# Two-layer mixer block in split fp32: partial-array products of a group issued without others between them, and another table of steps

## Chip, cores and metric

One core of a Trainium2 chip runs the whole block. The metric is the device time of one execution in microseconds. Three executions of the kernel before took 908.3, 911.97 and 912.93 us, with a median of 911.97 us.

## What is computed

Two layers over 256 tokens of width 1024, batch 1, all in fp32. A layer normalises x, multiplies by `w_in` and feeds three mixers: attention with 8 heads over compressed keys and queries (MLA), gated linear attention with 4 heads in chunks of 64 tokens (GLA), and a diagonal state-space mixer (S5) with 32 groups of 16 channels and 64 complex states each. Their outputs are gated and merged, go through `w_out`, and a feed-forward part with squared ReLU follows.

```python
for l in range(DEPTH):                       # 2
    z = rms_norm(x, norm1_g[l]) @ w_in[l]
    (cq, ckv, kpe, gq, gk, gv, glr, gr, su, gates) = split_in(z)
    o_a = mla_mixer(cq, ckv, kpe, ...)
    o_b = gla_mixer(gq, gk, gv, glr, gr, ...)
    o_c = s5_mixer(su, ...)
    g = sigmoid(gates + gate_b[l]).reshape(B, L, 3, D)
    merged = g[:,:,0]*(o_a@w_br_mla[l]) + g[:,:,1]*(o_b@w_br_gla[l]) + g[:,:,2]*(o_c@w_br_s5[l])
    x = x + merged @ w_out[l]
    x = x + square(relu(rms_norm(x, norm2_g[l]) @ w_ff1[l])) @ w_ff2[l]
```

## The kernel before

Every large product keeps fp32 accuracy by three products of rounded halves (`mm3`, L178 to L181): hi by hi, hi by lo, lo by hi. Weights stream in 128x1024 chunks (`raw`, by the SP queue); ScalarE rounds each into `hi` (L159) and VectorE takes the rest into `lo` (L160). These products use the whole 128x128 array.

The smaller products are plain fp32, and the hardware runs each such matmul of the program as two, so that a program's matmul is two in the trace (transposes are one). Several use only a part of the array:

- `s5_v` (L565 to L574): the S5 inputs `V`. 16 matmuls per call, two calls per layer (steps `v0`, `v2`). Each uses 64 of the 128 rows; those of strip 0 use the upper half of the rows and those of strip 1 the lower half, and the two halves can run side by side. A call takes all four PSUM tiles of the pool `acc`.
- `gla_core`, first part (L941 to L953): `Ap`, 8 matmuls per layer on 64 rows, in two halves as above. Third part (L975 to L998): `glo`, on 64 columns or on 64 rows by 64 columns. Between them `dS` (L967), in quarters of the array.
- `att_pv` (L856 to L877): after every second head, four matmuls into `po`, two heads on 64 columns each.
- `s5_y` (L610 to L637): `yp`, one product with `K` on the whole array, then 16 on 32 columns each, for each of four channel tiles; four strips of 32 columns can run side by side.

The order of the program is not written out. A layer's mixers are cut into steps (`table`, L1160), and `STEPS` (L1142) lists them, one string per layer; `P` is a part of `s5_pre` (layer 0 alone: layer 1's parts run in the feed-forward part of layer 0), and `~n` moves a step's priority by n instructions. A scheduler then places each instruction on its engine by its priority and by when it believes its operands and buffers to be ready. So it also puts whole-array products between those of one partial group. What it has written out, each engine then runs in order.

The names in the rows: `gp` are the products of the gates, `cp` those of the latents, `brp` of the branches, `fp` and `fo` of the feed-forward part, `s` and `PTp` scores and transposed probabilities of a head, `hT` and `goT` transposes. A shape like 64*128 is rows by columns of the array, and 64x128 what streams through.

Of the kernel before, what the change touches and what calls it, by code (L numbers as in the profile page):

```python
# [20 lines left out]
L = 256  # L21
NT = L // 128
# [15 lines left out]
# Columns of w_in by part.  # L38
# [7 lines left out]
# Weight chunks, one row of the packed array each: (name, columns used).  # L46
# [12 lines left out]
# Columns of the packed small parameters.  # L59
# [9 lines left out]
# Columns of the packed constants.  # L69
# [17 lines left out]
class Kern:  # L87
# [100 lines left out]
    def ws4(self, outs, ws):  # L188
        """Four column tiles; the second half of the rows comes last."""
# [25 lines left out]
    def exp(self, y, x, n):  # L215
        """exp of a small [128, n] tile: 2^k times the series of the rest."""
# [10 lines left out]
        # k + 127 in the lowest bits, shifted to where the exponent is  # L227
# [4 lines left out]
    def split(self, hi, lo, src, scale=None):  # L232
        """hi + lo == src * scale"""
# [80 lines left out]
    def s5_pre(self, l):  # L314
# [22 lines left out]
        # in turns of the two steps of a chunk: thi + tlo, thi with few enough bits for exact products  # L337
# [12 lines left out]
        # lam_bar, (lam_bar - 1) / lam  # L350
# [20 lines left out]
        # b_bar, lam_bar b_bar, c lam_bar; each comes without its zeros and is copied into a block-diagonal form  # L371
# [11 lines left out]
        def cmul(outr, outi, ar, ai, xr, xi, neg=False):  # L383
            """(xr + i xi)(ar + i ai); with neg the second output is negated"""
# [20 lines left out]
        # first row of a chunk: lam_bar b_bar, second: b_bar  # L405
# [19 lines left out]
        # operands of the input products  # L425
# [11 lines left out]
        # within a chunk  # L437
# [12 lines left out]
        # angle of the rotation by chunk  # L450
# [80 lines left out]
    def norm_rows(self):  # L531
        """The tokens' factors along the columns, in every row."""
# [32 lines left out]
    def s5_v(self, l, r):  # L565
        """The input products of two strips: they hold different rows of the array."""
        nc, s = self.nc, self.s5c[l]
        self.V = [[self.pt(f"V{i}", [128, 4, 128], tag="acc") for i in range(2)] for _ in range(2)]
        for i in range(2):
            for q in range(4):  # L570
                for rr in range(2):
                    rows = slice(64 * rr, 64 * rr + 64)
                    nc.tensor.matmul(self.V[rr][i][:, q, :], lhsT=s["Bt"][i][rows, 2 * q + r // 2, :],
                                     rhs=self.u2[r // 2][rows, q, :], start=True, stop=True)  # L574

    def s5_r(self, l, r):
# [17 lines left out]
        # the running sum, chunk by chunk of the four tiles (R is 0 at each first chunk)  # L594
# [5 lines left out]
        # the states take the place of this strip's cosines and sines  # L600
# [7 lines left out]
    def s5_y(self, l):  # L608
# [5 lines left out]
        for i in range(2):  # L614
            p = self.pt("yp", [128, 2, L])
            for qq in range(2):
                q = 2 * i + qq
                st = [slice(32 * r, 32 * r + 32) for r in range(4)]
# [737 lines left out]
```

## Time and profile before

| | |
|---|---|
| runs | 908.3, 911.97, 912.93 us; median 911.97 |
| the profiled execution | span 909.6 us; what lies around the span is not given, so the span stands for its own time |
| TensorE busy | 892.9 us, 98% of the span |
| VectorE / ScalarE busy | 674.7 us (74%) / 518.8 us (57%) |
| DMA | 147.78 MB, mean 162 GB/s |
| layer 0, mixers and `w_out` | about 12 to 270 us; feed-forward to about 460 us |
| layer 1 | mixers from about 460 us; feed-forward from about 720 us |

The profile counts TensorE as busy while any matmul is in flight, and matmuls overlap, so a busy share near 100% does not say how fast it goes. The distance from one start to the next does. The granted clock (PEclk) is 1.00 or 0.50 of 2.4 GHz in any one instant; a mean in between is a mix of the two.

### The profile page before, as it was taken

What the parts mean: (1) busy time and instruction counts of PE and PEld (TensorE: products, weight loads), DVE (VectorE), ACT (ScalarE), POOL (GpSimd) and SP (SyncE); (2) the same over time, 40 slices, a digit from 0 to 9 for tenths busy, and PEclk for the clock granted to TensorE, in tenths of its full rate; (3) what the DMA queues carried; (4) which work ended last, traced back from release to release, by engine and by line L of the source; (5) the groups of instructions that cost most, each with busy time, mean ns of one, the idle gap of its engine ahead of it and who ended that gap; (6) DMA issues with size and microseconds to landing.
All of it is one profiled execution on the core that took longest, in us unless ns stands there. A gap on an engine that the chain in (4) does not pass through costs nothing.

```text
span 909.6 us, 16218 instructions
## 1 busy us (share of the span) xinstructions
PE 892.9 (98%) x6428; PEld 813.0 (89%) x6428; DVE 674.7 (74%) x1283; ACT 518.8 (57%) x794; POOL 19.7 (2%) x35
## 2 busy tenths in 40 slices
PE   7999999999999999999999999999999999999998
PEld 6879988899989999999898899879999899999996
DVE  7999999977777966875686777968878765555554
ACT  6777888545555655654457557744445554444442
POOL 2000000010000000000000000000000000000000
PEclk9999999999999999999999999978999999999999
DMA  7535434346665565666645345323555556666662
GB/s 260 177 110 150 144 116 124 91 147 207 193 200 164 175 197 178 189 188 185 185 154 170 111 152 151 105 70 116 163 163 181 173 184 189 190 191 188 186 186 93
DMA packets 42266, 147.78 MB, mean 162 GB/s; under 512 B 4688, under 2 KB 5328, under 8 KB 42192
## 3 DMA queue, kind: packets, MB, share of 16 engines
q1 hardware_dynamic: 42192, 146.76, 52.3%
q8 instruction: 50, 0.82, 0.4%
q14 instruction: 24, 0.20, 0.1%
HBM read 145.70 MB, written 1.05 MB: 161 GB/s over the span
## 4 chain that ended last, share of the span: by engine, by line
PE 86%; DVE 5%; ACT 4%; DMA 2%; issue 1%; SPq 0%; ACTq 0%; DVEq 0%
PE fp L179 7%; PE fp L181 7%; PE fp L180 7%; PE fo L179 6%; PE fo L180 6%; PE fo L181 6%; PE gp L179 4%; PE gp L180 4%; PE gp L181 4%; PE brp L179 2%; PE brp L181 2%; DVE lo L160 2%; PE brp L180 2%; PE wo L179 2%; PE wo L180 2%; PE wo L181 2%
## 5 line engine op out<-in xcount | busy, mean ns | idle before, releaser
L160 DVE TENSOR_TENSOR lo<-raw,hi 128x1024 fp32r<-128x1024 f32 (+1 forms) x276 | 333.1, 1208 | 157.0 <-ACT hi L159 156.0
L159 ACT CAST hi<-raw 128x1024 fp32r<-128x1024 f32 (+1 forms) x276 | 286.0, 1037 | 285.3 <-PE fp L180 81.3
L179 PE MATMUL fp<-h,hi 128*128 128x256 f32 x512 | 145.2, 284 | 0.0
L180 PE MATMUL fp<-h,hi 128*128 128x256 f32 x512 | 145.0, 283 | 0.0
L181 PE MATMUL fp<-h,lo 128*128 128x256 f32 x512 | 144.9, 283 | 0.0
L179 PE MATMUL gp<-h,hi 128*128 128x256 f32 x384 | 112.0, 295 | 0.2 <-DVE gt L1043 0.2
L181 PE MATMUL gp<-h,lo 128*128 128x256 f32 x384 | 111.1, 292 | 0.0
L180 PE MATMUL gp<-h,hi 128*128 128x256 f32 x384 | 110.7, 291 | 0.0
L179 PE MATMUL fo<-hi,r 128*128 128x512 f32 x256 | 100.2, 391 | 0.0
L180 PE MATMUL fo<-lo,r 128*128 128x512 f32 x256 | 99.9, 390 | 0.0
L181 PE MATMUL fo<-hi,r 128*128 128x512 f32 x256 | 99.6, 389 | 0.0
L179 PEld LDWEIGHTS fp<-h,hi 128*128 128x128 f32 x512 | 98.2, 192 | 0.9
L180 PEld LDWEIGHTS fp<-h,hi 128*128 128x128 f32 x512 | 98.2, 192 | 0.9
L181 PEld LDWEIGHTS fp<-h,lo 128*128 128x128 f32 x512 | 98.2, 192 | 0.0
L179 PEld LDWEIGHTS gp<-h,hi 128*128 128x128 f32 x384 | 74.1, 194 | 3.0 <-issue 1.6
L180 PEld LDWEIGHTS gp<-h,hi 128*128 128x128 f32 x384 | 74.3, 195 | 2.0 <-issue 1.3
L181 PEld LDWEIGHTS gp<-h,lo 128*128 128x128 f32 x384 | 74.2, 195 | 2.1 <-issue 1.4
L181 PEld LDWEIGHTS fo<-hi,r 128*128 128x128 f32 x256 | 48.1, 188 | 10.2
L179 PEld LDWEIGHTS fo<-hi,r 128*128 128x128 f32 x256 | 48.2, 188 | 9.2
L180 PEld LDWEIGHTS fo<-lo,r 128*128 128x128 f32 x256 | 48.2, 188 | 8.9
L1046 ACT ACTIVATE gt<-gt,hgateb 128x256 f32<-128x256 f32 x48 | 21.7, 500 | 11.9 <-DVE gt L1043 11.9
L180 PE MATMUL wo<-lo,mh 128*128 128x512 f32 x64 | 25.3, 395 | 0.0
(403 smaller groups left out, 1820.5 us busy)
## 6 DMA issues: line engine op xcount, KB each, us to landing
raw<-wst SPq DMA_DIRECT2D x266, 512.0 KB, 3.9
raw<-wst SPq DMA_DIRECT2D x6, 384.0 KB, 3.0
x<-xin SPq DMA_DIRECT2D x4, 256.0 KB, 4.9
raw<-wst SPq DMA_DIRECT2D x4, 256.0 KB, 5.5
bc_raw<-bcin SPq DMA_DIRECT2D x4, 256.0 KB, 3.9
out_dram<-x SPq DMA_DIRECT2D x4, 256.0 KB, 2.0
par<-parin SPq DMA_DIRECT2D x2, 205.0 KB, 6.4
masks<-consts SPq DMA_DIRECT2D x1, 128.0 KB, 4.1
```

The costliest lines, as they stand in the source:

```text
L159: nc.scalar.copy(hi[:, h], raw[:, h])
L160: nc.vector.tensor_tensor(out=lo[:, h], in0=raw[:, h], in1=hi[:, h].bitcast(F32), op=ALU.subtract)
L179: mm(out, lhsT=lt[0], rhs=rt[0], start=start, stop=False)
L180: mm(out, lhsT=lt[0], rhs=rt[1], start=False, stop=False)
L181: mm(out, lhsT=lt[1], rhs=rt[0], start=False, stop=stop)
L1046: nc.scalar.activation(g[:, m, :], g[:, m, :], AF.Tanh, scale=0.5, bias=self.small[l]["gateb"][:, c:c + 1])
```

## The change

A helper, `together()`, opens a block in which TensorE's instructions keep the order in which they are written. It is put around `s5_v`, the first and third parts of `gla_core`, the products of `att_pv`, and those of `s5_y`. Inside, the order is written anew, the halves in turns and the higher one first. `glo` of the first token tile is one whole-array product instead of two of 64 columns. `s5_y` has both `K` products first and then walks the four strips. Both strings of `STEPS` are new. The comments are gone, and lines move by some 5 to 8. Cut to its core:

```diff
+    def together(self):
+        return self.tc.manual_schedule(engines={mybir.EngineType.PE})
...
     def s5_v(self, l, r):
-        for i in range(2):
-            for q in range(4):
-                for rr in range(2):
+        with self.together():
+            for i in (1, 0):
+                for q in range(4):
+                    for rr in (1, 0):
...
     def s5_y(self, l):
-            for qq in range(2):
-                q = 2 * i + qq
-                mm(p[:, qq, 0::2], lhsT=s["K0"][:, q, :], rhs=self.u[:, q, 0::2], start=True, stop=False)
-                for i2 in range(2):
-                    for r in range(4):
-                        mm(p[st[r], qq, 2::2], lhsT=C[2 + i2][:, q, r, :], rhs=X[i2][:, r, q, 0:127],
-                           start=False, stop=i2 == 1)
-                for i2 in range(2):
-                    for r in range(4):
-                        mm(p[st[r], qq, 1::2], lhsT=C[i2][:, q, r, :], rhs=X[i2][:, r, q, :],
-                           start=i2 == 0, stop=i2 == 1)
+            with self.together():
+                for qq in range(2):
+                    q = 2 * i + qq
+                    mm(p[:, qq, 0::2], lhsT=s["K0"][:, q, :], rhs=self.u[:, q, 0::2], start=qq == 0, stop=False,
+                       skip_group_check=True)
+                for c, x in (((1, slice(1, L, 2)), slice(0, 128)), ((3, slice(2, L, 2)), slice(0, 127))):
+                    for i2 in range(2):
+                        for qq in range(2):
+                            for r in range(4):
+                                q = 2 * i + qq
+                                mm(p[st[r], qq, c[1]], lhsT=C[c[0] - 1 + i2][:, q, r, :], rhs=X[i2][:, r, q, x],
+                                   start=False, stop=i2 == 1, skip_group_check=True)
...
     def att_pv(self, l, h):
-        for k in range(2):
-            for j, x in enumerate((self.PT0, PT)):
+        with self.together():
+            for k in range(2):
+                for j, x in ((1, PT), (0, self.PT0)):
...
     def gla_core(self, l):
-        for t in range(NT):
-            ts_ = slice(t * 128, (t + 1) * 128)
-            for m in range(2):
-                for o in range(2):
+        with self.together():
+            for t in range(NT):
+                ts_ = slice(t * 128, (t + 1) * 128)
+                for m in range(2):
+                    for o in (1, 0):
...
-                if t:
-                    for o in range(2):
-                        mm(p[o], lhsT=A[o], rhs=vh[o], start=True, stop=False)
-                else:
-                    for o in range(2):
-                        for n in range(2):
-                            mm(p[o][half[n]], lhsT=A[o][:, half[n]], rhs=vh[o], start=True, stop=n == 0)
-                for n in (2 * t, 2 * t + 1):
-                    if n:
+        with self.together():
+            for t in range(NT):
+                for m in range(2):
+                    c = (t * 2 + m) * 128
                     for o in range(2):
+                        h = (2 * m + o) * 128
+                        mm(self.gpo[o][:, t, m, :], lhsT=self.At[o][:, c:c + 128], rhs=self.gv[t][:, h:h + 128],
+                           start=(t, m) == (0, 0), stop=False, skip_group_check=True)
+            for n in range(1, 4):
+                for m in range(2):
...
     STEPS = [
-        "qk P~-60 kg P~60 P~-75 P~-30 gate~30 P P~-2 P gv su0 P su0~-30 gv~27 gv gv core P ckv core~-30 P~-30 "
+        "qk P~-60 kg P~68 P~-15 gv~42 gate~30 P P~-2 P~15 gv su0 P P~-30 su0~-30 gv gv core~-8 ckv core~-98 P "
...
```

What it moves, in three places. TensorE in layer 1, the second call of `s5_v` (`V`, strips 2 and 3), before:

```order
L573 MATMUL V_7062<-u_6547,Bt 128x128 x2
L179 MATMUL gp<-h_5302,hi 128x256
L573 MATMUL V_7064<-u_6547,Bt 128x128 x2
L180 MATMUL gp<-h_5303,hi 128x256
L573 MATMUL V_7062<-u_6547,Bt 128x128
L573 MATMUL V_7064<-u_6547,Bt 128x128
L181 MATMUL gp<-h_5302,lo 128x256
L573 MATMUL V_7062<-u_6547,Bt 128x128
L179 MATMUL gp<-h_5302,hi 128x256
L573 MATMUL V_7064<-u_6547,Bt 128x128
L180 MATMUL gp<-h_5303,hi 128x256
```

and with the change, where the two tiles of one component take turns four times, and then those of the other:

```order
L185 MATMUL gp<-h_5329,hi 128x256
L186 MATMUL gp<-h_5328,lo 128x256
L579 MATMUL V_7170<-u_6580,Bt 128x128
L579 MATMUL V_7168<-u_6580,Bt 128x128
...
L579 MATMUL V_7169<-u_6580,Bt 128x128
L579 MATMUL V_7167<-u_6580,Bt 128x128
...
L184 MATMUL gp<-h_5328,hi 128x256
```

Twelve places at which a product of the gates (or a transpose `PTp`) stood between two `V` are gone; at least ten products of the gates in a row now stand ahead of the group.

TensorE in layer 1, the first part of `gla_core`, before:

```order
L180 MATMUL gp<-h_5303,hi 128x256
L950 MATMUL Ap<-ep,en 128x128
L181 MATMUL gp<-h_5302,lo 128x256
L950 MATMUL Ap<-ep,en 128x128
L179 MATMUL gp<-h_5302,hi 128x256
L950 MATMUL Ap<-ep,en 128x128
L180 MATMUL gp<-h_5303,hi 128x256
```

and so on for eight `Ap`; with the change:

```order
L184 MATMUL gvp<-hi,h_5328 128x512
L185 MATMUL gvp<-lo,h_5328 128x512
L186 MATMUL gvp<-hi,h_5329 128x512
L960 MATMUL Ap<-ep,en 128x128 x8
L184 MATMUL gp<-h_5328,hi 128x256
```

All eight stand together. TensorE in layer 0, the second call of `s5_v`, before (the scores `s` of one head ahead of it):

```order
L840 MATMUL s<-kT,qT 128x128
L840 MATMUL s<-kT,qT 128x256
L573 MATMUL V_2047<-u_1479,Bt 128x128
L573 MATMUL V_2049<-u_1479,Bt 128x128
...
L862 MATMUL PTp<-con,ppt 128x128
L573 MATMUL V_2049<-u_1479,Bt 128x128
L573 MATMUL V_2048<-u_1479,Bt 128x128
L862 MATMUL PTp<-con,ppt 128x128 x2
```

and with the change:

```order
L848 MATMUL s<-kT,qT 128x128
L848 MATMUL s<-kT,qT 128x256
L848 MATMUL s<-kT,qT 128x128
L848 MATMUL s<-kT,qT 128x256
L579 MATMUL V_2093<-u_1515,Bt 128x128
L185 MATMUL gp<-h_96,hi 128x256
L579 MATMUL V_2091<-u_1515,Bt 128x128
...
L579 MATMUL V_2092<-u_1515,Bt 128x128
L186 MATMUL gp<-h_95,lo 128x256
...
L579 MATMUL V_2090<-u_1515,Bt 128x128
```

Here the block only keeps the order of its own products: others still stand between them, at two places, and the scores of two heads stand directly ahead.

## Rows read from the trace of the kernel before

**Rows 1.** The page: its first line, the busy time, share and instructions of TensorE, and the shares of the chain of work that ended last, by engine.

```profile
span 909.6 us, 16218 instructions
...
PE 892.9 (98%) x6428; PEld 813.0 (89%) x6428; DVE 674.7 (74%) x1283; ACT 518.8 (57%) x794; POOL 19.7 (2%) x35
...
PE 86%; DVE 5%; ACT 4%; DMA 2%; issue 1%; SPq 0%; ACTq 0%; DVEq 0%
```

**Rows 2.** Timeline of TensorE in layer 1, the beginning of the `Ap` group. Columns: start in us, length in us, engine, line, operation, tiles, array rows*columns, what streams, count.

```profile
493.18 0.28 PE L179 MATMUL gp<-h,hi 128*128 128x256 f32 x1
493.30 0.28 PE L180 MATMUL gp<-h,hi 128*128 128x256 f32 x1
493.51 0.48 PE L950 MATMUL Ap<-ep,en 64*128 64x128 f32 x2
493.93 0.39 PE L181 MATMUL gp<-h,lo 128*128 128x256 f32 x1
494.24 0.48 PE L950 MATMUL Ap<-ep,en 64*128 64x128 f32 x2
494.66 0.38 PE L179 MATMUL gp<-h,hi 128*128 128x256 f32 x1
```

**Rows 3.** Timeline of TensorE in layer 0, two runs of `V` and the products behind each; columns as in rows 2.

```profile
113.83 1.16 PE L573 MATMUL V<-u,Bt 64*128 64x128 f32 x8
114.92 0.50 PE L179 MATMUL gp<-h,hi 128*128 128x256 f32 x2
...
155.77 1.16 PE L573 MATMUL V<-u,Bt 64*128 64x128 f32 x14
156.86 0.39 PE L179 MATMUL gp<-h,hi 128*128 128x256 f32 x1
```

**Rows 4.** Busy time of TensorE in the stretches with partial products. Each stretch goes from the start of the last whole-array product ahead of a group to the start of the second one behind it. Columns: stretch and its length in us, busy us of TensorE (matmuls in flight), granted clock, DMA share, GB/s.

```profile
50.75:53.97 3.22, 2.99 (x22) 1.00 0.52 163
...
113.62:117.85 4.23, 4.12 (x40) 1.00 0.45 124
136.03:137.03 1.00, 1.00 (x6) 1.00 0.00 0
153.03:157.08 4.05, 3.81 (x38) 1.00 0.02 4
160.62:161.86 1.24, 1.24 (x13) 1.00 0.00 0
...
187.56:192.71 5.15, 5.15 (x124) 1.00 0.81 251
493.30:499.26 5.96, 5.96 (x28) 1.00 0.66 251
517.17:521.66 4.49, 4.49 (x52) 1.00 0.29 97
566.14:572.87 6.73, 5.74 (x49) 1.00 0.38 114
597.43:613.40 15.97, 15.97 (x57) 0.63 0.23 66
655.73:662.11 6.38, 6.38 (x141) 1.00 0.60 209
```

**Rows 5.** Busy time of all engines in four more stretches. Columns: stretch and length, then busy us of PE, PEld, DVE, ACT and POOL with their counts, granted clock, DMA share, GB/s.

```profile
20.00:187.00 167.00, 162.03 (x1273) 145.12 (x1272) 157.05 (x414) 123.07 (x218) 5.04 (x8) 1.00 0.44 132
...
595.40:601.70 6.30, 6.30 (x37) 4.17 (x35) 6.16 (x18) 3.46 (x9) 0.72 (x2) 1.00 0.29 83
601.74:618.80 17.06, 17.06 (x57) 13.03 (x58) 6.69 (x12) 4.66 (x12) 0.00 (x0) 0.50 0.11 31
...
499.33:502.74 3.41, 3.41 (x18) 3.41 (x18) 2.24 (x4) 0.91 (x2) 0.00 (x0) 0.50 0.09 6
```

**Rows 6.** Timeline of TensorE inside the stretch at half clock; columns as in rows 2.

```profile
604.46 0.79 PE L573 MATMUL V<-u,Bt 64*128 64x128 f32 x2
605.19 0.58 PE L179 MATMUL gp<-h,hi 128*128 128x256 f32 x1
605.70 0.79 PE L573 MATMUL V<-u,Bt 64*128 64x128 f32 x2
```

**Rows 7.** Timeline of TensorE in layer 0, the products `dS` on quarters of the array and the one behind them; columns as in rows 2.

```profile
57.38 1.09 PE L967 MATMUL dS<-gv,kN 64*64 64x128 f32 x24
58.40 0.50 PE L181 MATMUL grp<-hi,h 128*128 128x512 f32 x1
```

**Rows 8.** Timeline of VectorE in layer 0, its last write of a state strip; columns as in rows 2, without the array.

```profile
186.25 0.69 DVE L606 TENSOR_TENSOR sinT<-sinT,rot 128x512 f32<-128x512 f32 x1
```

**Rows 9.** Timeline of TensorE in layer 0, products `yp`; columns as in rows 2.

```profile
187.56 0.28 PE L181 MATMUL gp<-h,lo 128*128 128x256 f32 x1
187.77 0.30 PE L622 MATMUL yp<-cosT,cmat 128*32 128x127 f32 x1
...
189.64 0.40 PE L622 MATMUL yp<-sinT,cmat 128*32 128x127 f32 x8
189.86 0.40 PE L626 MATMUL yp<-cosT,cmat 128*32 128x128 f32 x8
```

**Rows 10.** What VectorE waited for in layer 0, 20 to 187 us, the first entry: who waited for whom, us in total, times, longest.

```profile
DVE lo L160 <- ACT hi L159: 5.8, 7, 1.5
```

**Rows 11.** What TensorE waited for in the whole span, one entry; columns as in rows 10.

```profile
PE po L870 <- ACT ppt L863: 1.0, 1, 1.0
```

More of the change, by code (lines that the diff above doesn't have):

```diff
@@ L568, in s5_v @@
         self.V = [[self.pt(f"V{i}", [128, 4, 128], tag="acc") for i in range(2)] for _ in range(2)]
-        for i in range(2):
-            for q in range(4):
-                for rr in range(2):
-                    rows = slice(64 * rr, 64 * rr + 64)
-                    nc.tensor.matmul(self.V[rr][i][:, q, :], lhsT=s["Bt"][i][rows, 2 * q + r // 2, :],
-                                     rhs=self.u2[r // 2][rows, q, :], start=True, stop=True)
+        with self.together():
+            for i in (1, 0):
+                for q in range(4):
+                    for rr in (1, 0):
+                        rows = slice(64 * rr, 64 * rr + 64)
+                        nc.tensor.matmul(self.V[rr][i][:, q, :], lhsT=s["Bt"][i][rows, 2 * q + r // 2, :],
+                                         rhs=self.u2[r // 2][rows, q, :], start=True, stop=True)
     def s5_r(self, l, r):
@@ L615, in s5_y @@
             p = self.pt("yp", [128, 2, L])
-            for qq in range(2):
-                q = 2 * i + qq
-                st = [slice(32 * r, 32 * r + 32) for r in range(4)]
-                mm(p[:, qq, 0::2], lhsT=s["K0"][:, q, :], rhs=self.u[:, q, 0::2], start=True, stop=False)
-                for i2 in range(2):
-                    for r in range(4):
-                        mm(p[st[r], qq, 2::2], lhsT=C[2 + i2][:, q, r, :], rhs=X[i2][:, r, q, 0:127],
-                           start=False, stop=i2 == 1)
-                for i2 in range(2):
-                    for r in range(4):
-                        mm(p[st[r], qq, 1::2], lhsT=C[i2][:, q, r, :], rhs=X[i2][:, r, q, :],
-                           start=i2 == 0, stop=i2 == 1)
+            st = [slice(32 * r, 32 * r + 32) for r in range(4)]
+            with self.together():
[10 more added lines that the diff above has]
+                                   start=False, stop=i2 == 1, skip_group_check=True)
             yield
@@ L945, in gla_core @@
         p = [self.pt("Ap", [128, NT, 2, 128]) for _ in range(2)]
-        for t in range(NT):
-            ts_ = slice(t * 128, (t + 1) * 128)
-            for m in range(2):
-                for o in range(2):
-                    mm(p[o][:, t, m, :], lhsT=self.kt[half[o], m, ts_], rhs=self.qt[half[o], m, ts_], start=True, stop=True)
+        with self.together():
[3 more added lines that the diff above has]
+                    for o in (1, 0):
+                        mm(p[o][:, t, m, :], lhsT=self.kt[half[o], m, ts_], rhs=self.qt[half[o], m, ts_],
+                           start=True, stop=True)
         for o in range(2):
@@ L976, in gla_core @@
         self.gpo = [self.pt("glo", [128, NT, 2, 128], tag="acc") for _ in range(2)]
-        for t in range(NT):
-            for m in range(2):
-                A = [x[:, (t * 2 + m) * 128:(t * 2 + m + 1) * 128] for x in self.At]
-                vh = [self.gv[t][:, (2 * m + o) * 128:(2 * m + o + 1) * 128] for o in range(2)]
-                p = [x[:, t, m, :] for x in self.gpo]
-                if t:
-                    for o in range(2):
-                        mm(p[o], lhsT=A[o], rhs=vh[o], start=True, stop=False)
-                else:
-                    for o in range(2):
-                        for n in range(2):
-                            mm(p[o][half[n]], lhsT=A[o][:, half[n]], rhs=vh[o], start=True, stop=n == 0)
-                for n in (2 * t, 2 * t + 1):
-                    if n:
-                        for o in range(2):
-                            mm(p[o][half[n % 2]], lhsT=self.qt[half[o], m, n * 64:(n + 1) * 64],
-                               rhs=S[m][half[o], n - 1, :], start=False, stop=True)
+        with self.together():
+            for t in range(NT):
+                for m in range(2):
+                    c = (t * 2 + m) * 128
+                    for o in range(2):
+                        h = (2 * m + o) * 128
[3 more added lines that the diff above has]
+                for m in range(2):
+                    for o in range(2):
+                        mm(self.gpo[o][half[n % 2], n // 2, m, :], lhsT=self.qt[half[o], m, n * 64:(n + 1) * 64],
+                           rhs=S[m][half[o], n - 1, :], start=False, stop=True, skip_group_check=True)
         for o in range(2):
```

4 lines of the change are left out of this document (2 added, 2 removed), and 24 rows, old and new, of the table STEPS.

## Prediction, made before the changed kernel was run

> **What bounds the kernel now.** The page comes first: TensorE is busy for 98% of the span and holds 86% of the chain that ended last [rows 1]. So time is won only where TensorE gets through its program in less time. Busy does not mean fast, though, so I read the timeline next, for the distance from start to start. A whole-array product of 256 columns follows the one before by 0.12 us (493.18 to 493.30) [rows 2]. A partial product takes 0.11 us on its part of the array: eight `yp` on four strips, so two to a strip, take 0.22 us (189.64 to 189.86) [rows 9].
>
> What costs time is the change between whole and partial use. In the `Ap` group one whole-array product and two partial ones fill the 0.73 us from 493.93 to 494.66 [rows 2]; 0.12 and twice 0.11 are work, and **0.39 us is the price of going in and out once**. Two halves of the array also overlap only where they take turns: eight `V` of one half take 1.09 us to the next start, and fourteen in turns take 1.09 us too [rows 3].
>
> The third thing is the clock. From 601.74 to 618.80 us the granted clock is 0.50, the 1.2 GHz level, and again from 499.33 to 502.74 [rows 5]. Before both falls TensorE had no gap: it was busy for 6.30 of 6.30 us ahead of 601.70 [rows 5], but with partial products and changes between them, and during the slow stretch it goes on alternating, now at 1.24 us a turn (604.46 to 605.70) [rows 6].
>
> VectorE is the second candidate. From 20 to 187 us it is busy for 157.05 of 167 us [rows 5], so layer 0's mixers have two bounds.
>
> **The change, part by part.** I take each stretch of [rows 4], subtract the whole-array products that the timeline shows in it, and set the rest against the order with the change: runs of partial products at 0.11 us per pair or strip turn, plus 0.39 us per run.
>
> Layer 1:
> - `Ap`: 5.96 us less nine whole products is 4.88. Eight pairs in one run are 0.88 + 0.39 = 1.27. Saved: 3.6 us.
> - `V`, second call: 15.97 us less seventeen whole products (2.1) is 13.9; the six `po` in it are worth 1.0 at the price of eight together (1.24 less 0.24). 12.9 remain, against sixteen pairs, 1.76 + 0.39 = 2.15. Saved: 10.7 us, some 6 of it from the half clock.
> - What follows at half clock, from the end of that stretch, 613.40, to 618.80 is 5.40 us [rows 4, 5] of whole products, which take half as long at 2.4 GHz: 2.7 us. The other slow stretch, 3.41 us [rows 5], gives 1.7 us.
> - `V`, first call: 6.73 us less six whole products and transposes (0.7) is 6.0; `po` in two pieces is 1.8 of it; 4.3 against 2.15. Saved: 2.1 us, 1.0 of which is a wait for ScalarE [rows 11].
> - `po`: in three pairs of heads the first product went ahead alone, for 1.00 less 0.24 = 0.76 us; the six behind are taken at the price of eight. All eight are together now. Saved: 2.3 us.
> - `glo`: 4.49 us less 0.35 is 4.1. Now sixteen whole-array products of 128 columns, 1.8 us, and 24 on quarters at the pace of `dS`, 24 in 1.02 us [rows 7], with 0.2 for going in: 3.0. Saved: 1.1 us.
> - `yp`: 6.38 less 0.24 is 6.1. Now eight `K`, 0.9, 128 strip products, 3.5, and three changes, 1.2: 5.6. Saved: 0.5 us.
>
> Together 24.7 us.
>
> Layer 0, from the same view: `Ap` 2.86 against two runs, 1.66, saves 1.2. `V`, first call, 3.63 against two runs, 2.54, saves 1.1; second call, 3.4 against three runs, 2.9, saves 0.4 to 0.5. `po` saves 2.3 in three pairs of heads; `glo` is taken as in layer 1, 1.1. `yp` is 4.9 against one run of 3.6, less 0.4 for four more `K` ahead of it: 0.9. Together **7.0 us**, and 31.7 us for both layers.
>
> Not all of it arrives. In layer 0 `yp` stands behind the last write of VectorE to the state strips (186.25 us, 0.69 long) [rows 8], and it starts at 187.77 [rows 9], under a microsecond after that write ends. VectorE has the same work ahead of that write as before, and only 10 us of idle time to give up from 20 to 187 us, 5.8 of which it spends waiting for ScalarE's rounded weights [rows 5, 10]. Six of the seven microseconds fall ahead of that point. Nothing shows how many VectorE can follow: none at the one end, all at the other. I take half, since the waits for weights end when TensorE frees the buffers, and that comes sooner: **3 us lost**. The Trainium skill, "TensorEngine Tiling (Array Packing)", section "PSUM Bottleneck", says that packing speeds TensorE up but not the emptying of PSUM, which may then bound. By that rule all six would go, and the time would be 3 us above my forecast; the trace agrees in so far as VectorE has little to spare in layer 0 [rows 5].
>
> In layer 1 a `V` group now stands as one block that needs all four `acc` tiles, and every product behind it waits too. No row shows such a wait; the nearest is 1.0 us for `po` [rows 11]. Between nothing and twice that for each of two groups I take the row: **2 us lost**.
>
> The new table of steps adds no instruction on any engine; the same weight chunks come in another order through the SP queue. I cost that at nothing: at 132 GB/s from 20 to 187 us [rows 5], against 251 in a short stretch [rows 4], the queue has room. If that cover goes, chunks are late one by one and show as waits of TensorE for `lo` or `hi`.
>
> Sum: 909.6 - 31.7 + 3 + 2 = 882.9 us on the profiled execution's span, which I take as its own time. The median of the runs is 2.4 us above it, so the forecast is **885.3 us**, with 882 to 890 as its own range.
>
> **Rivals.**
> - *Layer 0 follows fully and nothing new waits*: 909.6 - 31.7 + 2.4 = 880.3 us. For it: VectorE's idle time is larger than what is saved. Against it: the listing puts two heads' scores directly ahead of layer 0's second `V` group.
> - *The clock falls all the same.* The two slow stretches cost 8.5 and 1.7 us, half of their lengths [rows 5]; then 895.5 us. For it: the falls came without a gap on TensorE, so the cause may lie elsewhere than in the alternation. Against it: both falls stand right behind or in the two groups that alternate most. The Trainium skill, "TensorE: Matmul & The Clock Gate", section "Why this matters for your kernels", names idle gaps between bursts as what drops the throughput in mid-kernel. By that rule closing up the products changes nothing in the clock, and this rival's time holds; the rows ahead of 601.70 speak against the rule, as they show a fall with no gap.
> - *The halves do not overlap in the new order* (the higher one first, which no row shows): sixteen more products at 0.11 in each of four `V` groups and eight in each `Ap` group, 8.8 us: 894.1 us. Against it: fourteen in turns went at twice the pace of eight [rows 3].
> - *Nothing measurable is left*: the last two together, layer 0 without gain and one more microsecond of wait at each `V` group of layer 1: 885.3 + 10.2 + 8.8 + 3 + 2 = 909.3 us.
> - *Slower: the blocks wait.* Each of the four `V` groups stops TensorE until VectorE has read the scores that hold its `acc` tiles. It decides from 7.9 us a group on, where four waits eat 31.7 us; with 10 us each it is 909.6 - 31.7 + 40 + 2.4 = 920.3 us. For it: VectorE's 157 of 167 us. Against it: the longest such wait now is eight times shorter [rows 11], and in layer 1 products of the gates stand ahead.
>
> **How the numbers follow.** The forecast gets 0.45, layer 0 in full 0.20, the clock 0.17, no overlap 0.09, nothing left 0.05, slower 0.04. The range, 877 to 897 us, takes in the first four, with some microseconds below for waits that also go; about one in ten is outside. A measurement of this kernel can tell about 0.5% from no change. The first four cases lie below that bound, 907.4 us: faster 0.91, same 0.05, slower 0.04.
>
> **What would show it.** Right: `V` in layer 1 as runs of 32 in about 2 us; a granted clock of 1.00 from 480 us on; no `Ap` with a whole product in between in layer 1; TensorE idle for a few microseconds ahead of `V` or `yp` in layer 0, with VectorE as the releaser. Wrong: a stretch at 0.50 in layer 1; single `V` 0.11 us apart in turns; or TensorE idle for over 8 us in the mixers beyond what it was.

## The result, and the profile after

The changed kernel takes 888.21 us (median of four executions, 886.43 to 888.91) beside 910.28 us of the kernel before on the same chip: a ratio of 0.976, with a 95% interval of 0.973 to 0.979. The forecast was 885.3 us in 877 to 897, faster. The profiled execution took 888.1 us with a span of 886.3, so 1.8 us lie around the span.

The page of the changed kernel: its first line, TensorE, and the shares of the chain that ended last.

```profile
span 886.3 us, 16190 instructions
...
PE 866.6 (98%) x6412; PEld 798.4 (90%) x6412; DVE 672.6 (76%) x1283; ACT 518.9 (59%) x794; POOL 22.5 (3%) x35
...
PE 81%; DVE 12%; ACT 3%; issue 2%; DMA 2%; SPq 0%; DVEq 0%; ACTq 0%
```

Against [rows 1] TensorE is busy for 98% again, in a span 23.3 us shorter, and VectorE's share of the chain has gone from 5% to 12%. Where the time went is read from four groups. Timeline of TensorE with the change; columns as in rows 2, with the idle time ahead and its releaser in brackets.

```profile
46.58 1.71 PE L438 MATMUL Btp<-con,bbar 128*128 128x128 f32 x8 [2.16 <-issue]
...
489.02 0.39 PE L186 MATMUL gvp<-hi,h 128*128 128x512 f32 x1
489.34 1.16 PE L960 MATMUL Ap<-ep,en 64*128 64x128 f32 x16
490.43 0.39 PE L184 MATMUL gp<-h,hi 128*128 128x256 f32 x1
...
560.48 2.06 PE L579 MATMUL V<-u,Bt 64*128 64x128 f32 x32
563.12 0.68 PE L848 MATMUL s<-kT,qT 96*128 96x128 f32 x3 [0.59 <-DVE rot L596]
...
596.77 2.06 PE L579 MATMUL V<-u,Bt 64*128 64x128 f32 x32
598.75 0.39 PE L184 MATMUL gp<-h,hi 128*128 128x256 f32 x1
...
602.54 0.87 PE L879 MATMUL po<-ppt,v 128*64 128x256 f32 x8 [1.05 <-DVE rot L596]
...
614.59 0.36 PE L184 MATMUL gp<-h,hi 128*128 128x256 f32 x1 [0.17 <-DVE gt L1051]
```

`Ap` stands as 16 records from 489.34 to 490.43 where [rows 2] shows it two by two between whole products. The second `V` call takes 1.98 us to the next start; in [rows 6] one pair and one whole product took 1.24. Behind the first `V` call and ahead of the last `po` there are waits for VectorE of 0.59 and 1.05 us that were not there before. Windows of the changed kernel; columns as in rows 5.

```profile
488.90:490.65 1.75, 1.75 (x20) 1.28 (x19) 1.75 (x2) 1.33 (x3) 0.00 (x0) 1.00 0.74 176
509.91:513.27 3.36, 3.36 (x45) 3.03 (x43) 3.19 (x11) 1.87 (x4) 0.00 (x0) 1.00 0.41 145
560.07:563.31 3.24, 2.52 (x37) 2.15 (x35) 1.91 (x4) 3.18 (x6) 0.00 (x0) 1.00 0.37 142
596.56:598.98 2.42, 2.42 (x37) 2.17 (x36) 2.42 (x4) 1.86 (x2) 0.00 (x0) 1.00 0.38 152
601.22:603.57 2.35, 1.30 (x13) 0.87 (x11) 2.35 (x5) 0.12 (x1) 0.00 (x0) 1.00 0.84 255
612.67:614.78 2.11, 1.94 (x18) 1.44 (x17) 2.11 (x4) 1.96 (x3) 0.00 (x0) 1.00 0.32 126
634.72:638.75 4.03, 4.03 (x127) 3.70 (x125) 3.79 (x7) 2.33 (x2) 0.00 (x0) 1.00 0.70 250
46.84:50.26 3.42, 3.42 (x16) 3.13 (x15) 2.95 (x7) 3.33 (x9) 0.00 (x0) 0.50 0.00 0
480.00:880.00 400.00, 397.75 (x2931) 368.81 (x2930) 286.81 (x462) 218.56 (x326) 6.78 (x6) 1.00 0.53 164
...
595.00:615.00 20.00, 18.78 (x172) 17.60 (x171) 19.97 (x30) 9.76 (x17) 4.51 (x2) 1.00 0.42 132
```

The first seven answer to [rows 4]: `Ap` (first row) is now 1.75 us where it was 5.96, and the second `V` call (fourth row) 2.42 where it was 15.97. From 480 to 880 us the clock is 1.00, where [rows 5] had two stretches at 0.50. There is a new one in layer 0, at 46.84, right behind the stop of 2.16 us ahead of `Btp`. The last row is to be set beside the same window of the kernel before:

```profile
595.00:615.00 20.00, 20.00 (x79) 13.84 (x78) 10.47 (x25) 6.29 (x17) 0.72 (x2) 0.67 0.18 52
```

VectorE was busy for 10.47 of these 20 us and is now for 19.97. Before, 13.3 of these 20 us were at half clock, so TensorE also asked less of it there.

For the comparisons below the span is cut in two, by starts of TensorE's instructions: **layer 0** from the first `kgp` to the first `K0p` behind `w_out`, **layer 1** from there to the last product. One profiled execution of each:

| kernel | ratio to before, 95% | layer 0, us | layer 1, us | stretches at 0.50 |
|---|---|---|---|---|
| before | 1 | 315.9 | 561.9 | 499.33 to 502.74, 601.73 to 618.79 |
| change | 0.9763, 0.9734 to 0.9792 | 314.7 | 541.0 | 46.84 to 50.26 |
| grouped_old_table | 0.9859, 0.9842 to 0.9875 | 313.4 | 550.8 | 493.48 to 500.30 |
| new_table_only | 0.9927, 0.9912 to 0.9942 | 321.0 | 548.6 | 48.22 to 51.63 |
| one_group | 0.9877, 0.9861 to 0.9893 | 315.4 | 549.4 | 496.69 to 500.10 |
| no_turns | 0.9803, 0.9789 to 0.9818 | 314.9 | 543.4 | none |
| l0_vec_less | 0.9752, 0.9737 to 0.9766 | 313.8 | 540.9 | 48.02 to 51.44 |
| l1_vec_less | 0.9798, 0.9780 to 0.9815 | 313.7 | 544.5 | 615.52 to 618.93 |
| before_l0_vec_less | 1.0008, 0.9992 to 1.0024 | 315.4 | 560.4 | 495.49 to 502.32, 604.72 to 614.96 |
| l0_pool | 0.9816, 0.9799 to 0.9834 | 319.3 | 540.5 | 48.83 to 52.24, 134.16 to 137.58 |
| mixed | 0.9777, 0.9757 to 0.9798 | 314.9 | 540.8 | 88.97 to 92.38 |
| mixed_tuned | 0.9756, 0.9736 to 0.9777 | 313.4 | 540.9 | none |
| tmp1 | 0.9942, 0.9921 to 0.9963 | 323.3 | 542.4 | 93.95 to 97.36 |
| raw4 | 0.9906, 0.9887 to 0.9925 | 325.4 | 541.2 | 54.57 to 57.99, 92.12 to 98.95 |

So 20.9 of the 23.3 us come from layer 1, 1.3 from layer 0, and about 1 from what lies ahead of the first `kgp` (26.47 against 27.50 us). That last piece is not the change's doing as far as the rows show: `mixed` and `mixed_tuned`, whose layer 0 is the same program, have 27.67 and 26.27.

Layer 0 itself varies with the clock. The change and l1_vec_less run the same instructions there in the same order on TensorE and VectorE; with the stretch at 46.84 it takes 314.7 us, without one 313.7. One of the four executions of l0_pool took 2981.22 us, with no trace that says why, and its numbers here rest on the other three.

### The profile page after: what moved, and what is told of

Its sections match the earlier page's. It is cut to its first block, busy times and chain, and to the rows that moved or that the text cites. A ratio compares the mean times of both kernels' runs of the same rounds, so it can differ in the third digit from the quotient of the medians.

```text
span 886.3 us, 16190 instructions
## 1 busy us (share of the span) xinstructions
PE 866.6 (98%) x6412; PEld 798.4 (90%) x6412; DVE 672.6 (76%) x1283; ACT 518.9 (59%) x794; POOL 22.5 (3%) x35
## 3 DMA queue, kind: packets, MB, share of 16 engines
HBM read 145.70 MB, written 1.05 MB: 166 GB/s over the span
## 4 chain that ended last, share of the span: by engine, by line
PE 81%; DVE 12%; ACT 3%; issue 2%; DMA 2%; SPq 0%; DVEq 0%; ACTq 0%
PE fp L184 7%; PE fp L186 7%; PE fp L185 7%; PE fo L184 7%; PE fo L185 7%; PE fo L186 7%; DVE lo L165 4%; PE gp L184 3%; PE gp L185 3%; PE gp L186 2%; PE brp L184 2%; PE brp L186 2%; PE brp L185 2%; PE wo L186 2%; PE wo L184 2%
## 5 line engine op out<-in xcount | busy, mean ns | idle before, releaser
L165 DVE TENSOR_TENSOR lo<-raw,hi 128x1024 fp32r<-128x1024 f32 (+2 forms) x276 | 332.8, 1207 | 157.7 <-ACT hi L164 156.9
L164 ACT CAST hi<-raw 128x1024 fp32r<-128x1024 f32 (+2 forms) x276 | 285.9, 1037 | 278.4 <-PE fp L185 78.9
L184 PE MATMUL gp<-h,hi 128*128 128x256 f32 x384 | 109.8, 291 | 1.0 <-ACT ppt L858 0.8
L186 PE MATMUL gp<-h,lo 128*128 128x256 f32 x384 | 107.6, 286 | 0.0
L185 PE MATMUL gp<-h,hi 128*128 128x256 f32 x384 | 107.2, 285 | 0.0
L184 PEld LDWEIGHTS gp<-h,hi 128*128 128x128 f32 x384 | 72.7, 192 | 3.0 <-ACT ppt L858 1.0
L185 PEld LDWEIGHTS gp<-h,hi 128*128 128x128 f32 x384 | 72.5, 191 | 1.0 <-issue 0.5
L186 PEld LDWEIGHTS fo<-hi,r 128*128 128x128 f32 x256 | 48.1, 188 | 10.2
L184 PE MATMUL wo<-hi,mh 128*128 128x512 f32 x64 | 24.9, 395 | 0.0
```

The source lines that it names most:

```text
L164: nc.scalar.copy(hi[:, h], raw[:, h])
L165: nc.vector.tensor_tensor(out=lo[:, h], in0=raw[:, h], in1=hi[:, h].bitcast(F32), op=ALU.subtract)
L184: mm(out, lhsT=lt[0], rhs=rt[0], start=start, stop=False)
L185: mm(out, lhsT=lt[0], rhs=rt[1], start=False, stop=False)
L186: mm(out, lhsT=lt[1], rhs=rt[0], start=False, stop=stop)
```

## The experiments

**Which part of the change does it?** Two kernels take one part each.

```diff
 # grouped_old_table: the change, with the strings of before
-        "qk P~-60 kg P~68 P~-15 gv~42 ...
+        "qk P~-60 kg P~60 P~-75 P~-30 ...
 # new_table_only: before, with the strings of the change
-        "qk P~-60 kg P~60 P~-75 P~-30 ...
+        "qk P~-60 kg P~68 P~-15 gv~42 ...
```

> The changed kernel with the table of steps of the kernel before: the blocks that keep the order of a group, and the new orders inside them, without the new table. In its listing layer 1's Ap are again eight single products with a whole-array product between any two, and V comes in runs of 9 and 7 and of 1, 13 and 2; po, glo and yp are as in the change. Theory (what counts is which products stand side by side, by the sums of the prediction): against the change, Ap costs 3.6 us more, the V calls 0.4 and 0.8, and the half clock around Ap (1.7 us) may come back; so 892.5 to 895 us. Rival A (the table is a detail, the blocks do the work): within 2 us of the change, 886 to 890 us. Rival B (the table alone does it): 905 us or more.

It took 896.93 us (before 909.12), 2 us more than the theory's range and far from both rivals. Layer 1 gains 11.1 us of the 20.9. `Ap` is again in single pairs. Timeline of TensorE (columns as in rows 2), where the clock falls:

```profile
492.75 0.49 PE L960 MATMUL Ap<-ep,en 64*128 64x128 f32 x2
493.17 0.38 PE L185 MATMUL gp<-h,hi 128*128 128x256 f32 x1
493.48 0.79 PE L960 MATMUL Ap<-ep,en 64*128 64x128 f32 x2
494.20 0.58 PE L186 MATMUL gp<-h,lo 128*128 128x256 f32 x1
```

and the window of the slow stretch (columns as in rows 5):

```profile
493.48:500.30 6.82, 6.82 (x23) 5.25 (x23) 2.51 (x4) 1.95 (x3) 0.00 (x0) 0.50 0.24 83
```

The fall to the 1.2 GHz level comes in the middle of the alternation, with no gap ahead of it: a turn of one pair and one product takes 0.73 us before it and 1.23 behind. It lasted twice as long as the one in [rows 5], and `yp` stood in more pieces than the theory counted (6.7 us for its groups against 5.7); these two are the larger part of what it missed.

> The kernel before with the new table of steps and nothing else: no blocks, the orders inside the groups as before. In its listing layer 1's Ap stand eight in a row all the same, V in runs of 4 and 12 and of 16. Theory (what counts is which products stand side by side): the terms for Ap, V and the half clock in layer 1 (20.8 us together) arrive but for 0.4 us of a second run; glo (1.1), yp (0.5) and some of po (1 to 2) do not, and two tiles of the first V run are not in turns (0.4): against the change 3 to 4 us more, 891 to 893 us. Rival A (the blocks do the work): 905 us or more.

It took 902.75 us, 10 us more than the theory said and 2 less than rival A. Layer 1 gains 13.3 us, with `Ap` in one run and no slow stretch, as expected; but without the blocks `po` costs about 3 us, `yp` 2.7 and `glo` 1.1 more than in the change. Layer 0 is 5.1 us longer than before, which no theory had. So neither part alone does it: the table brings the products of a group side by side, and the blocks keep groups whole that the same table would break up. In layer 0 the new string is only harmless with the blocks.

**What is one group worth, and does the clock hang on it?**

```diff
 # one_group: before, with the order kept in this one call, and earlier
-        for i in range(2):
+        with self.together() if (l, r) == (1, 2) else self.later(0):
+            for i in range(2):
...
-        "h7 p6 g12 v2~-30 g13~60 ...
+        "h7 p6 g12 v2~-60 g13~60 ...
```

> The kernel before with one thing changed: the second call of V in layer 1 goes 30 instructions earlier and keeps its order, so that its 16 products stand as 1 and 15 where they stood in eleven pieces with products of the gates between. Nothing else moves but a few rows beside it. Theory (the pieces cost 0.39 us each time, and the alternation brings the clock down): 13.9 us of partial work becomes 3, and the half clock from 601.74 to 618.80 us is gone, which gives another 2.7 us behind the group: 12 to 13.5 us less than before, 896.8 to 898.3 us beside a median of 910.3, with a granted clock of 1.00 from 510 us on. Rival A (the clock falls all the same): the price of the pieces alone, about 6 us, 904 us, with a stretch at 0.50 near 605 us. Rival B (the pieces are hidden by other bounds): no change.

It took 897.98 us, 11.1 less than before; layer 1 is 12.5 us shorter. Timeline of TensorE, the group (columns as in rows 2):

```profile
597.25 2.05 PE L577 MATMUL V<-u,Bt 64*128 64x128 f32 x30
```

and windows of the same kernel (columns as in rows 5), the stretch at `Ap`, which was left in pieces, and everything behind:

```profile
496.69:500.10 3.41, 3.41 (x17) 3.23 (x17) 2.65 (x5) 1.04 (x3) 0.00 (x0) 0.50 0.00 0
510.00:880.00 370.00, 368.69 (x2715) 341.21 (x2714) 263.08 (x411) 199.44 (x299) 5.94 (x6) 1.00 0.55 166
```

Some thirty rows of TensorE's program moved, the long slow stretch is gone, and the one at `Ap` stays. Rival A, 904 us, is out. This is the main experiment: closing up this one group gives 11.1 us, half of what the whole change gives. The other kernels bear this out. In the four whose `Ap` of layer 1 stand in pairs between whole products (before, one_group, before_l0_vec_less, grouped_old_table) the clock falls in that group or right behind it, and in none of the ten others; it falls at the second `V` call only in the two that have it in single pairs (before, before_l0_vec_less).

**Do the halves overlap only in turns?**

```diff
 # no_turns: the change, in V (and in Ap, with o outermost)
-            for i in (1, 0):
-                for q in range(4):
-                    for rr in (1, 0):
+            for rr in (1, 0):
+                for i in (1, 0):
+                    for q in range(4):
```

> The changed kernel with the halves of the array not in turns: in V all products of one strip and then all of the other, in Ap all of one half and then all of the other. Groups stay together. Theory (two halves overlap only in turns; sixteen more products at 0.11 us in each of four V groups, eight in each of two Ap groups, and layer 0's share of 4.4 us partly taken up by the waits for VectorE): 4.4 us more than the change at the least, 8.8 at the most, so 892.6 to 897 us, and each V run of layer 1 takes 3.8 us instead of 2.1. Rival (the halves do not overlap anyway, or overlap in any order): within 1 us of the change, V runs of layer 1 of the same length.

It took 891.35 us, about 3.1 more than the change (the intervals of the two ratios just touch; its shortest execution, 890.96, is longer than the longest of the change, 888.91). Timeline of TensorE, the two `V` calls of layer 1:

```profile
561.36 3.50 PE L579 MATMUL V<-u,Bt 64*128 64x128 f32 x32
...
598.42 3.50 PE L579 MATMUL V<-u,Bt 64*128 64x128 f32 x32
```

The run takes 3.50 us instead of 2.06, so the halves do overlap in turns, the higher one first as well. The sum was too large: behind the first call TensorE no longer waits for VectorE (0.59 us in the change), so only 0.8 us of its 1.4 arrive. Layer 0 shows 0.3 us beside the change, but it has no stretch at 0.50 here; beside the 313.7 us of the change's layer 0 without one, it is 1.2.

**Did VectorE take what layer 0 should have gained?**

```diff
 # l0_vec_less (of the change) and before_l0_vec_less: != 0; l1_vec_less: != 1
+        if l != 0:
-        tt(out=m[0], in0=m[0], in1=m[1], op=ALU.add)
-        tt(out=m[2], in0=m[2], in1=m[3], op=ALU.subtract)
+            tt(out=m[0], in0=m[0], in1=m[1], op=ALU.add)
+            tt(out=m[2], in0=m[2], in1=m[3], op=ALU.subtract)
```

> The changed kernel without the two sums of VectorE ahead of the running sum, in layer 0 alone, so that the states there are not the ones asked for: 8 instructions of 0.68 us less on VectorE, 5.5 us, nothing less on TensorE. Theory (VectorE sets the pace of layer 0, and took what the grouping saved there): the main run of yp starts 3 to 5.5 us sooner than at 184.79 us, and the whole is 3 to 5 us shorter than the change, 883 to 885 us. Rival (TensorE or the order of its program sets the pace of layer 0): within 1 us of the change.

It took 887.3 us: the ratio cannot be told from that of the change, and layer 0 is 313.8 us. Timelines of VectorE and TensorE, the last write of a state strip and the beginning of the main run of `yp`, first in the change, then here:

```profile
184.40 0.68 DVE L612 TENSOR_TENSOR sinT<-sinT,rot 128x512 f32<-128x512 f32 x1
184.79 0.52 PE L634 MATMUL yp<-cosT,cmat 128*32 128x128 f32 x9
...
178.86 0.68 DVE L613 TENSOR_TENSOR sinT<-sinT,rot 128x512 f32<-128x512 f32 x1
180.20 0.52 PE L635 MATMUL yp<-cosT,cmat 128*32 128x128 f32 x9
```

VectorE is done 5.5 us sooner and `yp` starts 4.6 us sooner, as the theory said, but the layer does not end sooner by that: TensorE then has other products left over. With a stretch at 0.50 in either, layer 0 is 0.9 us shorter than in the change; against the change's layer 0 without one it is no shorter. So VectorE holds `yp`, but its amount of work does not set the pace of layer 0. One thing is not kept fixed: the scheduler also gave TensorE another order in layer 0 (the second `V` call stands in one run of 32 here).

> The same 5.5 us of VectorE work left out in layer 0 of the kernel before. Theory (layer 0 has two bounds close to each other, and the pieces of TensorE's groups cost less than they seem, since VectorE was no further): some gain, 1 to 4 us, but less than in the changed kernel, because TensorE's pieces then bound it; the difference between the two is what the grouping is worth in layer 0 once VectorE has room, 2 to 5 us instead of the 1.3 us now. Rival A (VectorE alone set layer 0's pace already before): as much as in the changed kernel. Rival B (TensorE alone set it): none.

909.23 beside 909.04 us: none, as rival B had it. With it falls the expected 2 to 5 us of grouping "once VectorE has room": layer 0 is 315.4 us here and 313.8 in the change with the same relief, 1.6 us where it is 1.3 without.

> The same 5.5 us of VectorE work left out in layer 1 alone, where VectorE is not asked for more than it can give: both theories expect the time of the change within 1 us (two waits of TensorE for these strips, 0.6 and 1.05 us in the change, may go, which would be up to 1.6 us). If it is 3 us or more, VectorE bounds layer 1 as well and the sums of the prediction for layer 1 rest on the wrong engine.

891.52 us, slower than the change by 3.3 us, which neither theory had (the intervals of the ratios overlap; the executions do not, with 889.73 us the shortest here and 888.91 the longest of the change, and layer 1 is 3.5 us longer). Timeline of TensorE:

```profile
613.24 0.41 PE L635 MATMUL yp<-cosT,cmat 128*32 128x128 f32 x4
615.53 0.55 PE L184 MATMUL gp<-h,hi 128*128 128x256 f32 x1 [1.88 <-DVE gt L1052]
```

and of VectorE:

```profile
612.48 2.33 DVE L604 TENSOR_TENSOR_SCAN rot<-R,rot 128x512 f32<-128x512 f32 x2
614.73 0.66 DVE L1052 TENSOR_TENSOR gt<-gp,rb 128x512 f32<-128x512 f32 x1
```

The step that frees the tile of the next gate product, `gt`, stands on VectorE behind two running sums, and TensorE waits 1.88 us for it; behind the stop the clock falls for 3.4 us. In the change the same `gt` stands behind single products, and TensorE waits 0.17 us for it. So VectorE had less to do in all, and TensorE waited longer at this place: the place of one instruction in VectorE's queue made this wait. The whole 3.5 us are not shown to be its work, since the scheduler changed TensorE's order in layer 1 as well (the last `po` stand in three pieces).

```diff
 # l0_pool: the change
+        t0 = nc.gpsimd.tensor_tensor if l == 0 and r < 3 else tt
-        tt(out=m[0], in0=z[0], in1=co, op=ALU.mult)
-        tt(out=m[2], in0=z[1], in1=si, op=ALU.mult)
+        t0(out=m[0], in0=z[0], in1=co, op=ALU.mult)
+        t0(out=m[2], in0=z[1], in1=si, op=ALU.mult)
```

> The changed kernel with six products of VectorE in layer 0 (two for each of the first three strips, 0.68 us each, 4.1 us) done by GpSimd, which is busy for 3% of the span; nothing is left out. GpSimd takes 1.34 us for a copy of 128x512, so 1.5 to 3 us for such a product, with the strip's next step waiting for it. Theory (VectorE sets layer 0's pace, and GpSimd's work runs beside it): 2 to 4 us shorter than the change, 884 to 886 us. Rival A (the two slow each other down, or the strip's chain waits for GpSimd): the same or up to 5 us longer. Rival B (TensorE sets the pace): within 1 us.

893.63 us, with layer 0 longer by 4.7: rival A. About 1 us of it may be the second stretch at half clock, at 134.16. Timeline of GpSimd:

```profile
126.31 2.03 POOL L608 TENSOR_TENSOR rot<-rot,cosT 128x512 f32<-128x512 f32 x1 [90.43 <-DVE rot L603]
128.31 2.27 POOL L609 TENSOR_TENSOR rot<-rot,sinT 128x512 f32<-128x512 f32 x1
...
147.56 1.29 POOL L608 TENSOR_TENSOR rot<-rot,cosT 128x512 f32<-128x512 f32 x1 [15.27 <-DVE arec L861]
```

and of VectorE at the same time:

```profile
127.20 2.23 DVE L165 TENSOR_TENSOR lo<-raw,hi 128x1024 fp32r<-128x1024 f32 x1
...
129.91 1.76 DVE L165 TENSOR_TENSOR lo<-raw,hi 128x1024 fp32r<-128x1024 f32 x1
...
133.82 1.22 DVE L165 TENSOR_TENSOR lo<-raw,hi 128x1024 fp32r<-128x1024 f32 x1
```

A `lo` that takes 1.22 us alone takes 2.23 and 1.76 beside GpSimd's product, and that takes 2.03 and 2.27 instead of 1.29. The Trainium skill, "SBUF — State Buffer", section "SBUF: two separate sides", says that a VectorE operation with two SBUF inputs and a GpSimd operation that reads SBUF hold the ports they share exclusively, for the whole instruction. The rows agree to within 0.13 us: the first `lo` begins at 127.20, GpSimd's product ends at 128.34, and 1.22 us more would end at 129.56, where it ends at 129.43.

**Can the parts be put together better?** `mixed` has the change's blocks, the old string for layer 0 and the new one for layer 1. `mixed_tuned` also moves two steps of layer 1.

```diff
 # mixed_tuned, on top of mixed
-        ... v0~-132 s0~-8 g11 h2 g00 ...   g20~15 p7 g20~60
+        ... v0~-132 s0~-8 g11 h2~30 g00 ...   g20~15 p7~15 g20~60
```

> The blocks as in the change, the old string of steps for layer 0 and the new one for layer 1. Layer 0, from the first product for kpe and the gate's latent to the first K0p of the feed-forward part, takes 313.3 us with the old string and the blocks, 314.7 with both new, and 315.9 in the kernel before. Theory (the two layers are independent; layer 0 gains from the blocks alone, and nothing from its new string, which moves a stop of 2.3 us to 44 us and brings a stretch of 3.4 us at half clock behind it): 1 us or a little more below the change, 886 to 888 us, with no stretch at 0.50 ahead of 880 us. Rival (layer 0's new string is worth something that the profile of one execution does not show): 889 us or more.

888.64 us: not below the change. The stop ahead of `Btp` is shorter (1.44 us instead of 2.16), but in this execution the clock fell at 88.97 us, where the same layer 0 in two other kernels (grouped_old_table, mixed_tuned) had no fall and took 1.5 us less (313.4). With the blocks, layer 0's strings are worth the same: 313.4 and 313.7 us without a fall, 314.9 and 314.7 with one.

> As the run with the old string for layer 0 and the new one for layer 1, and in layer 1 two steps put later: the scores of head 2 by 30, the transposes and po of head 7 by 15 instructions, so that eleven and fifteen products of the gates stand where TensorE stopped behind the first and second V group (0.59 us ahead of s, 1.05 us ahead of po; both waits for VectorE to read V). Theory (these are the waits that the blocks brought into layer 1, and they are worth what they are long): 1.6 us less than that run, 884.5 to 886.5 us, both waits gone. Rival (VectorE reads V no sooner, and the wait turns up at the next product that needs a tile): the same as that run within 0.5 us.

886.68 us, 2.0 less than `mixed` and 0.2 above the theory's range, but for another reason. Timeline of TensorE:

```profile
612.94 0.38 PE L184 MATMUL gp<-h,hi 128*128 128x256 f32 x1 [1.21 <-DVE gt L1051]
```

Both waits went, but a `gp` now waits 1.21 us for VectorE's `gt` (0.17 in the change) and a transpose `PTp` waits 0.90 us for ScalarE instead of 0.28. Layer 1 is as long as in `mixed` (540.9 against 540.8 us). What differs between the two profiles is layer 0, 1.5 us by the stretch at half clock, and what lies ahead of the first `kgp`, 1.4 us; neither comes from the two moved steps. So the rival's mechanism fits: VectorE is full there (19.97 of 20 us in the change), and the waits taken away turn up at the next products. Against the change the intervals overlap, so no version here is shown to beat it.

**Is it the ring of weight buffers?** `tmp1` has one buffer for the tiles named `tmp` instead of three; `raw4` spends the room on a fourth for the weights.

```diff
-    NSM = {"gv": 2, "v": 2, "gt": 2, "tmp": 3}
+    NSM = {"gv": 2, "v": 2, "gt": 2, "tmp": 1}
-    NRAW = 3
+    NRAW = 4    # raw4 alone
```

> The changed kernel with one buffer instead of three for the small tiles named tmp. It frees 4 KB a partition and is only there to be set beside the run that spends them on a fourth buffer for the incoming weights. Both theories: the change or up to 3 us slower, since squares and masks now wait for one another.

> The same with one buffer for tmp, and four instead of three for incoming weight chunks. In layer 0 of the change ScalarE waits 0.4 and 1.3 us for chunks at 124 and 127 us, and SP cannot ask for a chunk before VectorE has taken the rest (lo) from the one that holds the buffer. Theory (layer 0 is held back by this ring, in which VectorE's place in its queue counts and not its sum of work): 2 to 4 us shorter than the run with one tmp buffer and three for the weights, the waits of ScalarE for raw gone at 118 to 132 us. Rival (what holds TensorE in layer 0 are chains of small steps, row maximum, exponential, reciprocal, transposes, whatever the chunks do): within 1 us of that run.

902.98 and 900.24 us. The base already lost 15 us against the change, much more than expected and mostly in layer 0 (323.3 us), and raw4 has 10.2 us at half clock in layer 0, so the pair does not tell. The 2.7 us between the two medians lie in the theory's range, but not where it put them: in the profiled executions layer 0 is 2.1 us longer with the fourth buffer (325.4 us), and the waits of ScalarE for `raw` at 118 to 132 us are gone in both. Inconclusive.

## Why the prediction was right, and where not

- **TensorE bounds and the price of going in and out is 0.39 us: right.** In layer 1 the price of each group came out as forecast: `Ap` 1.29 us (forecast 1.27), second `V` call 2.18 (2.15), `glo` 3.01 (3.0), `yp` 1.87 + 3.79 = 5.66 (5.6), each by the window less its whole products (0.12 us for 256 columns, 0.23 for 512).
- **The clock: right.** No stretch at 0.50 in layer 1, the 2.7 and 1.7 us arrive. one_group and grouped_old_table show that the stretches go and come with the alternation, not with the rest of the kernel. What the prediction did not have is a new fall in layer 0, at 46.84. It and the one at 615.52 in l1_vec_less stand right behind stops of TensorE, of 2.16 and 1.88 us; yet no_turns and l1_vec_less have the same stop ahead of `Btp` (2.16 and 2.15 us) and no fall behind it, so what decides there stays open. The Trainium skill, "TensorE: Matmul & The Clock Gate", section "Why this matters for your kernels", names idle gaps; the falls at 493.48 and 601.73 have no gap ahead.
- **The new waits in layer 1: right in size, 1.6 us (0.59 + 1.05) for 2 forecast.** The first `V` call and the last `po` cost that much more than their terms. In mixed_tuned both were moved away and layer 1 became no shorter. Layer 1 is shorter by 20.9 us where 24.7 - 2 = 22.7 were forecast; the terms as measured give about 22.8 (waits included), so some 1.9 us are not placed.
- **Layer 0: the term of 7.0 us was a little too large, and the clock was not in it.** Sorted by start-to-start distances between the two marks, the groups take some 6.4 us less, the whole products 1.3 more (the stretch at 0.50 lies among them), and the waits some 3.6 more. How a distance is sorted is in part a choice, which moves these differences by some 0.2 us. The second `V` call did not become cheaper (3.8 us against 2.9 forecast and 3.4 before), since two products of the gates still stand in it and a transpose behind it waits 0.49 us for ScalarE.
- **The deduction of 3 us in layer 0: near in size, by luck, and wrong in its reason.** TensorE's waits there grew by some 3.6 us by the same sorting; the profile's own count of idle time, which leaves out what is hidden behind records that still run, grew from 4.85 to 6.67. But the sign that the prediction named, TensorE idle ahead of `V` or `yp` in layer 0 with VectorE as the releaser, did not appear: the longest waits are 2.16 us ahead of `Btp` and 1.12 us ahead of a `PTp`, for ScalarE. The prediction took the start of `yp` for the pace of the layer. VectorE does hold `yp`, yet with `yp` 4.6 us sooner in l0_vec_less the layer was at most 0.9 us shorter. By the rule of "TensorEngine Tiling (Array Packing)", section "PSUM Bottleneck", of the Trainium skill the time would have been 888.3 us, almost what was measured, but the two kernels with less VectorE work speak against emptying tiles as the mechanism in layer 0. In layer 1, where the prediction had not looked for it, VectorE is full, 19.97 of 20 us; but only some 6 of these read PSUM (`V`, `gt`, `oa`), so this is not the rule at work by itself.
- **Layer 0's outcome, 1.3 us instead of 4.0, is the larger part of the miss.** Layer 1 adds 1.8 us to it, and the 1.0 us ahead of the first `kgp`, which no term had, takes some away; with 0.5 us from the step between span and median (2.4 taken, 1.9 measured) that makes the 2.9 us. About 1.0 of layer 0's 2.7 is the stretch at half clock in the profiled execution. What exactly holds TensorE there stays open. The rows name single waits (2.16 us ahead of `Btp`, while VectorE works through the products `z` from which ScalarE fills `bbar`, and some 2 us for the first heads' softmax); l1_vec_less shows in layer 1 that the place of one small instruction in VectorE's queue can cost such a wait. That it is this in layer 0 was not shown.
- **"The new table costs nothing": wrong as it was put.** In layer 0 the new string without the blocks costs 5.1 us. With them it is neutral. The prediction credited the blocks with the grouping; with the old strings the blocks give 11.1 of layer 1's 20.9 us, and the rest needs the table.
- **Halves in turns: right**, and smaller in effect than the rival's 8.8 us, because behind a shorter run TensorE waits for VectorE.
- **One rival's sum has a slip.** In "nothing measurable is left", layer 0 without gain is put at 3 us, but the forecast credits layer 0 with 4.0 (7.0 less 3). Nothing hangs on it.

## What to carry to other kernels

Look for partial-array products that alternate with whole ones: a turn cost 0.39 us here at full clock, and in layer 1 the long alternations were where the clock came down, which then slowed what stood behind. Keeping a group in order is not keeping it together: look in the listing at what the scheduler puts between. Before a gain is counted, ask of the stretch it falls in which engine comes next; where that is full, as VectorE was here, a wait taken away can come back at the next product.

## What the runs showed of the hardware that was not expected

- The granted clock fell with TensorE busy and no gap, in the middle of alternating partial and whole products (493.48 us in grouped_old_table). The kernel before had a mean clock of 0.984 to 0.992 in every execution beside the experiments; the change had 0.998 to 1.000.
- Short falls come and go between executions of the same layer 0: 46.84 us in one kernel and none in another (314.7 against 313.7 us), 88.97 us in `mixed` and none in `mixed_tuned` (314.9 against 313.4). A difference of 1 to 1.5 us between two profiles can come with that alone.
- GpSimd's product of two tensors nearly doubles a VectorE product that runs at the same time (2.23 against 1.22 us), so GpSimd was no help to a full VectorE in this kernel.
